# The head of a two-branch decoder layer: a first slice of one row tile, its modulation spread over column tiles, and bursts of four row tiles set among the transposes of x

## The chip, the cores and the metric

The kernel runs on one core of one Trainium2 chip. The metric is device time in microseconds of one execution. In the profile PE is TensorE (PEld its weight loads), DVE VectorE, ACT ScalarE, POOL GpSimd, and SP the queue from which nearly all weights are loaded.

## The reference

One layer is computed for 256 prompt tokens and 8 x 8 sample tokens that share all weights: T = 320 columns of tokens. What matters here is its beginning:

```
mod = jax.nn.silu(c) @ w_ada + b_ada
sh1, sc1, g1, sh2, sc2, g2 = [m[:, None, :] for m in jnp.split(mod, 6, axis=-1)]

h = _rmsnorm(x, norm1_g) * (1 + sc1) + sh1
p = h @ w_in
...
q, k, v, og, u, ga, gb, alr = jnp.split(p, idx, axis=-1)
```

c is one vector for the prompt and one for each of the 8 sample sequences, so 9 rows. D_MODEL is 2048: 16 row tiles of 128 channels. After p come gated linear attention in 4 heads, a pooling branch, a merge with w_o, and an FFN of inner width 5632. All in 32-bit floats.

## The kernel before

**Layout.** Activations lie transposed: channels on partitions, 320 tokens along the row. h has 16 row tiles, hh[k] (high part) and hl[k] (low part). A weight is split as well, into whi (a cast on ACT, L149) and wlo (a subtraction on DVE, L150), and each product is three matmuls of 320 columns (mm3, L163 to L165). A *unit* is 256 columns of w_in: two matmul groups, so 6 matmuls for each row tile of h. Its result lies in one of two PSUM tiles ("pm", two buffers) until `evac` copies it out.

**Slices.** h can't be formed at once, since each row tile needs its part of sh1 and sc1, and these need their columns of w_ada. So the first 15 units (all 11 of head 0, and 4 of gb for heads 1 and 3) are made slice by slice over row tiles: (0, 2), (2, 4), (4, 8), (8, 12), (12, 16). Each slice adds to what the ones before have left in SBUF. In slices of two row tiles, units with 512 neighbouring columns are made in pairs from one load (proj_pair). While a slice runs, the modulation and h of the next one are made in the background: a list `bg` of steps, of which `after_unit` runs as many as the count of units done so far asks for. The order of the steps is the order in which they are issued.

**Modulation.** HeadJob(b0, s) makes sh1 and sc1 of s row tiles. w_ada is the moving operand and silu(c) the weights (9 of 32 rows): 4 column tiles of PE work side by side, each on 64 s columns of w_ada. `load(k0)` issues two pieces of 512 KB (sections 0 and 1) for nk = 8 / s row tiles of w_ada; a *burst* (`burst(k0)`) first issues the loads of up to two bursts ahead and then runs its matmuls (ada_mm, L215). The pieces lie in eight buffers (tag "araw"). `finish` copies the sums to adasb, transposes them back and adds b_ada.

**Queues.** All loads of w_ada and w_in are issued on SP in program order (raw_chunk, L139; they are pinned with keep_in_program_order). A load waits there until its buffer is free, and those behind it wait too. w_in has three buffers (tag "raw"), the split parts five each. Other instructions are put in order by a scheduler unless they are pinned.

**The head.** c is transposed and turned into silu (scT); x (two tiles of the prompt, one of the samples) is loaded on SP, and its 16 row tiles are transposed on PE (L126) and copied out (L455); the sums of squares (ACT, L469) become rx, the inverse norm of each token on all partitions, by a matmul of a diagonal (dg, L477). Then comes HeadJob(0, 2), h of row tiles 0 and 1 (h_unit, L483 to L492), and the slices.

Of the kernel before, what the change touches and what calls it, by code (L numbers as in the profile page):

```python
# [11 lines left out]
F32 = mybir.dt.float32  # L12
# [8 lines left out]
P = 128  # L21
# [3 lines left out]
D = 2048  # L25
# [13 lines left out]
SLICES = ((0, 2), (2, 4), (4, 8), (8, 12), (12, 16))  # L39
# [41 lines left out]
def body(tc, A):  # L81
# [17 lines left out]
    def misc():  # L99
        return pmisc.tile([P, 512], F32, tag="m", name=nm("pm"))  # L100
# [23 lines left out]
    def tr(out, in_):  # L124
        k = in_.shape[0]
        PE.transpose(out, in_, ident[:k, :k])  # L126
# [26 lines left out]
    def split_chunk(src, nk, nn):  # L153
# [13 lines left out]
    def proj(w, col, k0, k1, xh, xl):  # L167

        ps = pmain.tile([P, 2, 512], F32, tag="pm", name=nm("ps"))
        for c0 in range(k0, k1, 4):  # L170
            nk = min(4, k1 - c0)
            for j, whi, wlo in split_chunk(w[:, c0:c0 + nk, col:col + 256], nk, 256):
# [21 lines left out]
    def proj_pair(w, col, k0, k1, xh, xl):  # L194

        parts = list(split_chunk(w[:, k0:k1, col:col + 512], k1 - k0, 512))
# [15 lines left out]
    def ada_mm(ps, k, raws, w):  # L212

        for j in range(4):
            ins = PE.matmul(ps[32 * j:32 * j + 32, 0:w], lhsT=scT[:, k, :], rhs=raws[j], start=k == 0,  # L215
                            stop=k == KT - 1, tile_position=(0, 32 * j))
            if j == 0:
                tc.keep_in_program_order(ins)
# [153 lines left out]
    with tc.tile_pool(name="head", bufs=1) as xp:  # L372
# [8 lines left out]
        nc.sync.dma_start(xn[2][0:TS], A["x_sample"].rearrange("b t d -> (b t) d"))  # L381
# [15 lines left out]
        V.tensor_tensor(scT[:, :, 0:9], crT, csig, op=ALU.mult)  # L397

# [3 lines left out]
        class HeadJob:  # L402
# [7 lines left out]
            def load(self, k0):  # L410
                if k0 >= KT or k0 in self.raws:
                    return
                c = self.b0 * P
                self.raws[k0] = [raw_chunk(wada[:, k0:k0 + self.nk, sec * D + c:sec * D + c + self.s * P], self.nk,
                                  self.s * P, xp, "araw", 8) for sec in range(2)]

            def burst(self, k0):
                for ahead in range(3):
                    self.load(k0 + ahead * self.nk)
                raws = self.raws[k0]  # L420
                self.raws[k0] = None
                if self.ps is None:
                    self.ps = misc()
                w = self.w
                for i in range(self.nk):
                    ada_mm(self.ps, k0 + i, [raws[j // 2][:, i, (j % 2) * w:(j % 2) * w + w] for j in range(4)], w)

            def finish(self):
                nb = self.s // 2
                sb = xp.tile([P, 2 * P], F32, tag="adasb", name=nm("adasb"))  # L430
                S.copy(sb[:, 0:self.w], self.ps[:, 0:self.w])
# [4 lines left out]
                for sec in range(2):  # L436
                    blk = sec * KT + self.b0
                    ada_out(mod[:, blk:blk + self.s, :], src[:, 2 * sec:2 * sec + 2, :, 0:9], blk, (2, nb))

            def steps(self):  # L440
                return ([lambda: self.load(0)] + [lambda k0=k0: self.burst(k0) for k0 in range(0, KT, self.nk)]
                        + [self.finish])


        xT = []
        for k in range(KT):
            pt = misc()
            for i in range(3):
                n = P if i < 2 else TS
                tr(pt[:, i * P:i * P + n], xn[i][:n, k * P:(k + 1) * P])  # L450
# [4 lines left out]
            (S.copy if k % 2 else V.tensor_copy)(xT[k], pt[:, 0:T])  # L455

        pt = misc()
# [7 lines left out]
        ssq = xp.tile([P, 3], F32, name="ssq")  # L465
        V.memset(ssq, 1.0)
        for i in range(3):
            n = P if i < 2 else TS
            S.activation(junk[:n], xn[i][:n], AF.Square, accum_out=ssq[:n, i:i + 1])  # L469
# [9 lines left out]
        V.tensor_copy(rx, prs[:, 0:T])  # L479

# [41 lines left out]
        for f in HeadJob(0, SLICES[0][1]).steps():  # L522
            f()
        for k in range(SLICES[0][1]):
            h_unit(k)
        for si, (k0, k1) in enumerate(SLICES):
            bg = []
            acc = 0 if si == 0 else 1
            if si + 1 < len(SLICES):
# [5 lines left out]
                bg += HeadJob(n0, n1 - n0).steps()  # L535
# [22 lines left out]
            while e < len(early):  # L558
                ge, kind, i, col = early[e]
                if k1 - k0 == 2 and kind not in "qku":  # L560
# [572 lines left out]
```

## Time and profile before

| what | us |
|---|---|
| median of 3 runs | 2017.34 |
| lowest and highest | 2016.09 to 2018.74 |
| the profiled execution | 2013.89 |
| its span, first to last instruction | 2012.1 |
| PE busy in it | 1958.5 |

The span is that of the profiled execution alone; the rest of its time lies around the span. In rows of a timeline the columns are start, duration, engine, line, operation, tiles and shape, and in brackets the idle time before and what ended it. In rows of windows they are the stretch, its length, busy time (and count) of PE, PEld, DVE, ACT and POOL, the granted clock of PE, the DMA share and GB/s. In rows of DMA issues they are the count, the size and the median time from issue to landing.

### The profile page before, as it was taken

To read this page: it belongs to the slowest core of one execution; us is meant where nothing else is said; L and a number is where in the kernel's file an instruction comes from. 1 tells how busy PE (TensorE), PEld (TensorE's weight loads), DVE (VectorE), ACT (ScalarE), POOL (GpSimd) and SP (SyncE) were. 2 spreads that over 40 slices of the span, in tenths; PEclk is the share of its full clock that TensorE was granted. 3 is DMA by queue.
4 is the path that set the end of the run, shared out by engine and by line. 5 is a ranking of instruction groups with operands and counts; after the bars stand their busy time and mean duration, and the time that the engine had idled before them with its cause. 6 is when DMAs were issued, how large, how long until landed. Compare 5 with 4: busy or idle time off the path is not lost.

```text
span 2012.1 us, 37187 instructions
## 1 busy us (share of the span) xinstructions
PE 1958.5 (97%) x15008; PEld 1851.2 (92%) x15008; DVE 1015.4 (50%) x1881; ACT 819.7 (41%) x1466; POOL 140.0 (7%) x261
## 2 busy tenths in 40 slices
PE   7999999999999999999989999999999999999997
PEld 5889998888898899888979999999999999999997
DVE  2556665465546433665574344444444444444554
ACT  4333374354335333643344333333333343444443
POOL 1112220111001100110020000000000000000000
PEclk9999999999999999999989999999999999999998
DMA  8888755776975887569736666544444554454442
GB/s 292 287 297 272 232 158 152 251 246 193 311 242 157 275 270 229 159 222 353 233 106 217 210 201 205 172 147 150 150 152 148 153 152 147 149 155 143 150 143 90
DMA packets 319598, 400.83 MB, mean 199 GB/s; under 512 B 13529, under 2 KB 259801, under 8 KB 319089
## 3 DMA queue, kind: packets, MB, share of 16 engines
q1 hardware_dynamic: 307154, 358.21, 56.1%
q0 software_dynamic: 12272, 40.25, 5.6%
q8 instruction: 117, 1.92, 0.4%
q14 instruction: 55, 0.45, 0.1%
HBM read 373.96 MB, written 24.67 MB: 198 GB/s over the span
## 4 chain that ended last, share of the span: by engine, by line
PE 92%; DMA 4%; DVE 1%; ACT 1%; issue 1%; SPq 0%; POOL 0%; ACTq 0%; POOLq 0%; DVEq 0%
PE ps L163 27%; PE ps L164 27%; PE ps L165 27%; PE pm L215 4%; DMA raw<-w_in 2%; PE pm L126 2%; DMA raw<-w_ada 2%; PE pm L797 1%; PE pm L766 1%; PE pm L818 1%; DVE wlo L150 1%; DMA xn<-x_sample 1%; PE pm L793 0%; PE pm L755 0%; PE pm L638 0%
## 5 line engine op out<-in xcount | busy, mean ns | idle before, releaser
L150 DVE TENSOR_TENSOR wlo<-raw,whi 128x512 fp32r<-128x512 f32 x952 | 659.4, 697 | 836.1 <-ACT whi L149 825.9
L149 ACT CAST whi<-raw 128x512 fp32r<-128x512 f32 x952 | 586.8, 621 | 1016.3 <-PE ps L164 868.6
L163 PE MATMUL ps<-hh,whi 128*128 128x320 f32 x1408 | 445.9, 317 | 6.9 <-ACT whi L149 2.8
L163 PE MATMUL ps<-h2h,whi 128*128 128x320 f32 x1408 | 437.6, 311 | 5.1 <-ACT h2h L1039 5.1
L165 PE MATMUL ps<-hh,wlo 128*128 128x320 f32 x1408 | 442.3, 314 | 0.3
L164 PE MATMUL ps<-hl,whi 128*128 128x320 f32 x1408 | 440.7, 313 | 0.4 <-DVE hl L492 0.4
L164 PE MATMUL ps<-h2l,whi 128*128 128x320 f32 x1408 | 435.2, 309 | 0.0
L165 PE MATMUL ps<-h2h,wlo 128*128 128x320 f32 x1408 | 435.2, 309 | 0.0
L163 PEld LDWEIGHTS ps<-hh,whi 128*128 128x128 f32 x1408 | 266.8, 190 | 30.2 <-issue 15.3
L165 PEld LDWEIGHTS ps<-hh,wlo 128*128 128x128 f32 x1408 | 266.9, 190 | 8.4 <-issue 5.7
L163 PEld LDWEIGHTS ps<-h2h,whi 128*128 128x128 f32 x1408 | 265.3, 189 | 9.3 <-ACT h2h L1039 6.1
L164 PEld LDWEIGHTS ps<-hl,whi 128*128 128x128 f32 x1408 | 266.9, 190 | 7.1 <-issue 5.4
L164 PEld LDWEIGHTS ps<-h2l,whi 128*128 128x128 f32 x1408 | 265.3, 188 | 0.0
L165 PEld LDWEIGHTS ps<-h2h,wlo 128*128 128x128 f32 x1408 | 265.2, 188 | 0.0
L163 PE MATMUL ps<-ah,whi 128*128 128x320 f32 x704 | 217.7, 309 | 0.0
L165 PE MATMUL ps<-ah,wlo 128*128 128x320 f32 x704 | 216.5, 308 | 0.0
L164 PE MATMUL ps<-al,whi 128*128 128x320 f32 x704 | 216.5, 308 | 0.0
L164 PEld LDWEIGHTS ps<-al,whi 128*128 128x128 f32 x704 | 132.0, 187 | 0.0
L163 PEld LDWEIGHTS ps<-ah,whi 128*128 128x128 f32 x704 | 132.0, 187 | 0.0
L165 PEld LDWEIGHTS ps<-ah,wlo 128*128 128x128 f32 x704 | 131.9, 187 | 0.0
L215 PE MATMUL pm<-raw,scT 128*32 128x128 f32 (+1 forms) x2688 | 110.6, 297 | 8.1 <-DMA raw<-w_ada 8.1
L215 PEld LDWEIGHTS pm<-raw,scT 128*32 128x32 f32 x2688 | 69.9, 111 | 35.9 <-issue 20.2
(279 smaller groups left out, 1539.6 us busy)
## 6 DMA issues: line engine op xcount, KB each, us to landing
raw<-w_ada SPq DMA_DIRECT2D x192, 512.0 KB, 6.0
raw<-w_gu SPq DMA_DIRECT2D x176, 512.0 KB, 3.6
raw<-w_in SPq DMA_DIRECT2D x173, 512.0 KB, 4.2
raw<-w_down SPq DMA_DIRECT2D x80, 512.0 KB, 3.4
S<-state_gla POOLq DMA_DIRECT2D x16, 1024.0 KB, 8.4
o_gs<-S POOLq DMA_DIRECT2D x16, 1024.0 KB, 5.7
raw<-w_o SPq DMA_DIRECT2D x32, 512.0 KB, 4.8
raw<-w_down SPq DMA_DIRECT2D x16, 256.0 KB, 2.6
```

The costliest lines, as they stand in the source:

```text
L126: PE.transpose(out, in_, ident[:k, :k])
L149: S.copy(hi, raw)
L150: V.tensor_sub(lo, raw, hi.bitcast(F32))
L163: PE.matmul(ps, lhsT=whi, rhs=xhi, start=start, stop=False)
L164: PE.matmul(ps, lhsT=whi, rhs=xlo, start=False, stop=False)
L165: PE.matmul(ps, lhsT=wlo, rhs=xhi, start=False, stop=stop)
L215: ins = PE.matmul(ps[32 * j:32 * j + 32, 0:w], lhsT=scT[:, k, :], rhs=raws[j], start=k == 0, stop=k == KT - 1, tile_position=(0, 32 * j))
L766: PE.matmul(pt, lhsT=E["kdn"][:, s, d * P:(d + 1) * P], rhs=E["vn"][:, s], start=s == 0, stop=s == 1)
L797: PE.matmul(pt[32 * j:32 * j + 32, :], lhsT=qeP[:, d, 4 * gg + j, :], rhs=E["S0", gg, d][:, j], start=False, stop=d == 1, tile_position=(0 ...
L818: PE.matmul(pt, lhsT=kpz[:, gg, j, d * P:(d + 1) * P], rhs=E["vp"][:, gg], start=True, stop=True)
```

## The change

The slices become (0, 1), (1, 3), (3, 7), (7, 11), (11, 16). The first has a job of its own kind, HeadJob1: one row tile, sections 0 and 1 and the two halves of the 16 row tiles of w_ada on the four column tiles, so that the halves are added afterwards; it is used for the last row tile too. A burst now always covers four row tiles. It issues the loads for itself and the next burst, runs its matmuls, and then issues the loads two bursts ahead. The first job's bursts are set among the transposes of x, which are pinned now with their copies; the last four row tiles are transposed in the first slice. The w_in pieces of the first five loads are split in program order around h of row tile 0. x_sample is loaded from POOL's queue, and Sqrt's table is loaded early by a dummy activation.

```diff
-SLICES = ((0, 2), (2, 4), (4, 8), (8, 12), (12, 16))
+SLICES = ((0, 1), (1, 3), (3, 7), (7, 11), (11, 16))
...
+        def hi(self):
+            tc.keep_in_program_order(S.copy(self.h, self.raw))
+
+        def lo(self):
+            tc.keep_in_program_order(V.tensor_sub(self.l, self.raw, self.h.bitcast(F32)))
...
-        nc.sync.dma_start(xn[2][0:TS], A["x_sample"].rearrange("b t d -> (b t) d"))
+        nc.gpsimd.dma_start(xn[2][0:TS], A["x_sample"].rearrange("b t d -> (b t) d"))
...
+        warm = xp.tile([P, 1], F32, name="warm")
+        S.activation(warm, csig[:, 0, 0:1], AF.Sqrt)
...
             def load(self, k0):
+
                 if k0 >= KT or k0 in self.raws:
                     return
                 c = self.b0 * P
-                self.raws[k0] = [raw_chunk(wada[:, k0:k0 + self.nk, sec * D + c:sec * D + c + self.s * P], self.nk,
-                                  self.s * P, xp, "araw", 8) for sec in range(2)]
+                self.raws[k0] = [[raw_chunk(wada[:, k:k + self.nk, sec * D + c:sec * D + c + self.s * P], self.nk,
+                                            self.s * P, xp, "araw", 8) for sec in range(2)]
+                                 for k in range(k0, k0 + 4, self.nk)]
 
             def burst(self, k0):
-                for ahead in range(3):
-                    self.load(k0 + ahead * self.nk)
-                raws = self.raws[k0]
+
+                self.load(k0)
+                self.load(k0 + 4)
+                pieces = self.raws[k0]
...
+                todo = [(p, i) for p in reversed(range(4 // self.nk)) for i in range(self.nk)]
+                for n, (p, i) in enumerate(todo):
+                    ada_mm(self.ps, k0 + p * self.nk + i,
+                           [pieces[p][j // 2][:, i, (j % 2) * w:(j % 2) * w + w] for j in range(4)], w,
+                           k0 == 0 and n == 0, k0 == KT - 4 and n == 3)
+                self.load(k0 + 8)
...
+        class HeadJob1:
...
+            def load(self, q):
+                if q in self.raws:
+                    return
+                c = self.b0 * P
+                self.raws[q] = [raw_chunk(wada[:, 8 * (j % 2) + 4 * q:8 * (j % 2) + 4 * q + 4,
+                                               (j // 2) * D + c:(j // 2) * D + c + P], 4, P, xp, "araw", 8)
+                                for j in range(4)]
...
+            def steps(self):
+                return [lambda: (self.load(0), self.load(1)), lambda: self.burst(0), lambda: self.burst(1), self.finish]
...
-        for f in HeadJob(0, SLICES[0][1]).steps():
-            f()
-        for k in range(SLICES[0][1]):
-            h_unit(k)
+        nx = SLICES[0][1]
+        for q, n in ((0, 8), (1, 10)):
+            job0.burst(q)
+            while len(xT) < n:
+                x_trans(len(xT), len(xT) % 2)
+        ew = []
+        for kind, i, col in units(0)[:6]:
+            if kind == "v" and i == 1:
+                continue
+            n = 512 if kind in ("v", "og") else 256
+            ready[col] = [EarlySplit(raw_chunk(win[:, 0:nx, col:col + n], nx, n))]
+            ew += ready[col]
+        ew[0].hi()
+        job0.finish()
+        h_first(0)
+        for k in (10, 11):
+            x_trans(k, 1)
+        ew[0].lo()
+        for e in ew[1:]:
+            e.hi()
+            e.lo()
...
-                bg += HeadJob(n0, n1 - n0).steps()
+                if si == 0:
+                    bg += [lambda k=k: x_trans(k, k % 2) for k in range(12, KT)]
+                b = n0
+                while b < n1:
+                    size = 4 if n1 - b >= 4 else 2 if n1 - b >= 2 else 1
+                    bg += (HeadJob(b, size) if size > 1 else HeadJob1(b)).steps()
+                    b += size
```

What this does to the order, at two places. The first is SP in the slice of four row tiles that comes third, (4, 8) before and (3, 7) now, from the first w_ada piece of its job on. The number behind raw tells the pieces apart; w_ada pieces are background, w_in pieces are units. Before:

```order
L139 DMA raw_1304<-w_ada 128x2x512
L139 DMA raw_1306<-w_ada 128x2x512
L139 DMA raw_1309<-w_in 128x4x256
L139 DMA raw_1344<-w_ada 128x2x512
L139 DMA raw_1346<-w_ada 128x2x512
L139 DMA raw_1348<-w_ada 128x2x512
L139 DMA raw_1350<-w_ada 128x2x512
L139 DMA raw_1362<-w_in 128x4x256
L139 DMA raw_1397<-w_ada 128x2x512
L139 DMA raw_1399<-w_ada 128x2x512
L139 DMA raw_1410<-w_in 128x4x256
L139 DMA raw_1447<-w_ada 128x2x512
```

The ninth piece of w_ada (raw_1447) takes over the buffer of the first (raw_1304). Now, from the fourth and last piece of the first load on:

```order
L139 DMA raw_1192<-w_ada 128x2x512
L139 DMA raw_1195<-w_in 128x4x256
L139 DMA raw_1231<-w_in 128x4x256
L139 DMA raw_1268<-w_ada 128x2x512
L139 DMA raw_1270<-w_ada 128x2x512
L139 DMA raw_1272<-w_ada 128x2x512
L139 DMA raw_1274<-w_ada 128x2x512
L139 DMA raw_1293<-w_ada 128x2x512
L139 DMA raw_1295<-w_ada 128x2x512
L139 DMA raw_1297<-w_ada 128x2x512
L139 DMA raw_1299<-w_ada 128x2x512
L139 DMA raw_1302<-w_in 128x4x256
```

raw_1293 to raw_1299 take over the buffers of the job's first four pieces, raw_1186 to raw_1192, and raw_1302 stands behind them. PE at the same place now, from the last rows of the burst that reads these four pieces to the first matmuls of the unit made of raw_1302 (whi_1304 and wlo_1305 are its first halves):

```order
L241 MATMUL pm_1276<-raw_1186,scT 32x256 x2
L241 MATMUL pm_1276<-raw_1188,scT 32x256 x2
L188 MATMUL ps_1301<-hh_88,whi_1304 128x320
L189 MATMUL ps_1301<-hl_965,whi_1304 128x320
L190 MATMUL ps_1301<-hh_88,wlo_1305 128x320
```

The burst stands directly ahead of that unit. Before, two units and two bursts stood between the burst that reads raw_1304 and the unit whose w_in piece comes behind raw_1447.

The second place is ACT at the start of the first slice. Before, the casts of the w_in pieces stood wherever the scheduler put them (raw_474 is the fourth piece, u's):

```order
L149 CAST whi_390<-raw_388 128x512
L149 CAST whi_410<-raw_408 128x512
L431 COPY adasb_360<-pm_291 128x128
L149 CAST whi_433<-raw_431 128x512
L149 CAST whi_437<-raw_431 128x512
L487 ACTIVATE hh_85<-xh_367,mod 128x256
L488 CAST hh_85<-xh_367 128x64
L487 ACTIVATE hh_86<-xh_377,mod 128x256
L488 CAST hh_86<-xh_377 128x64
L149 CAST whi_476<-raw_474 128x512
L346 ACTIVATE q_274<-ps_387 128x640
```

Now (raw_296 is q's piece, raw_300 k's, raw_304 v's, raw_308 u's):

```order
L166 CAST whi_298<-raw_296 128x256
L576 ACTIVATE hh_85<-xh_226,mod 128x256
L579 CAST hh_85<-xh_226 128x64
L534 COPY xT_337<-pm_333 128x320
L534 COPY xT_343<-pm_339 128x320
L166 CAST whi_302<-raw_300 128x256
L166 CAST whi_306<-raw_304 128x512
L166 CAST whi_310<-raw_308 128x256
L373 ACTIVATE q_228<-ps_354 128x640
```

The casts of k's and v's pieces now follow h of row tile 0 and two copies of transposes, and u's cast still stands ahead of q's copy. raw_308 takes over the buffer of raw_296, as there are three.

More of the change, by code (lines that the diff above doesn't have):

```diff
@@ L454, in body @@
                 xT.append(hp.tile([P, T], F32, tag="hl%d" % k, name="xT%d" % k))
-            (S.copy if k % 2 else V.tensor_copy)(xT[k], pt[:, 0:T])
+            pinned((S.copy if eng else V.tensor_copy)(xT[k], pt[:, 0:T]))
+        job0 = HeadJob1(0)
+        for q in range(2):
+            job0.load(q)
+        ssq = xp.tile([P, 3], F32, name="ssq")
+        V.memset(ssq, 1.0)
+        for i in range(3):
+            n = P if i < 2 else TS
+            S.activation(junk[:n], xn[i][:n], AF.Square, accum_out=ssq[:n, i:i + 1])
+        for k in range(SLICES[0][1]):
+            x_trans(k, 0)
         pt = misc()
```

90 lines of the change are left out of this document (70 added, 20 removed).

## The prediction

> **What bounds the kernel now.** I read the page first, then the timeline of the engines over the first 38 us, then the chain of waits, the clock by windows, and SP's own timeline where TensorE (PE) still waits later. The page:
>
> ```profile
> span 2012.1 us, 37187 instructions
> PE 1958.5 (97%) x15008; PEld 1851.2 (92%) x15008; DVE 1015.4 (50%) x1881; ACT 819.7 (41%) x1466; POOL 140.0 (7%) x261
> PE 92%; DMA 4%; DVE 1%; ACT 1%; issue 1%; SPq 0%; POOL 0%; ACTq 0%; POOLq 0%; DVEq 0%
> ```
>
> PE is the bound. The change takes no matmul away, so it can gain or lose only where PE waits, runs at a lower clock or switches between column tiles and full matmuls. The timeline of PE in the head:
>
> ```profile
> 10.45 1.12 PE L126 MATMUL pm<-cst,xn 128*128 128x128 f32 x4 [2.29 <-DMA xn<-x_prompt]
> 12.73 0.69 PE L126 MATMUL pm<-cst,xn 64*128 64x64 f32 x4 [1.16 <-DMA xn<-x_sample]
> 13.68 11.07 PE L126 MATMUL pm<-cst,xn 128*128 128x128 f32 x36 [0.26 <-DVE xT L455]
> 24.89 1.73 PE L477 MATMUL pm<-dg,cst 128*128 128x128 f32 x6
> 26.55 4.49 PE L215 MATMUL pm<-raw,scT 128*32 128x128 f32 x80
> 31.29 1.59 PE L215 MATMUL pm<-raw,scT 128*32 128x128 f32 x48
> 33.30 0.33 PE L126 MATMUL pm<-cst,adasb 128*128 128x128 f32 x1 [0.42 <-ACT adasb L431]
> 37.25 0.42 PE L164 MATMUL ps<-hl,whi 128*128 128x320 f32 x1 [0.39 <-DVE hl L492]
> ```
>
> Twelve row tiles of transposes take 11.07 us, 0.92 each. From 37.25 the main stream runs. Its matmuls start 0.15 us apart, but for a while 0.27 apart, as the chain and the windows show (the granted clock stands behind POOL, GB/s last):
>
> ```profile
> 40.49 0.27 PE ps L163
> 71.36 0.15 PE ps L164
> 34.90:38.30 3.40, 1.61 (x9) 1.35 (x10) 3.18 (x8) 1.72 (x5) 3.32 (x7) 1.00 0.99 304
> 38.30:41.70 3.40, 3.40 (x15) 3.40 (x14) 0.34 (x1) 0.37 (x1) 1.32 (x3) 0.50 1.01 309
> 41.70:45.10 3.40, 3.40 (x24) 3.33 (x23) 0.00 (x0) 1.74 (x3) 0.00 (x0) 0.99 1.04 399
> 1031.60:1045.20 13.60, 6.97 (x23) 6.07 (x24) 10.84 (x24) 6.17 (x19) 7.01 (x19) 0.50 0.03 8
> 14.40:17.80 3.40, 3.40 (x12) 1.78 (x12) 1.10 (x3) 3.15 (x8) 0.00 (x0) 1.00 1.09 386
> ```
>
> After a stretch of 3.4 us in which PE was half idle the granted clock is 0.50 for the next 3.4, and it comes back after a full one; behind the long idle time at 1031 it takes 13.6. At half clock 1 - 0.15/0.27 = 0.45 of the time is lost. The 1.00 at 14.4 is no record: the 80 column matmuls at 26.55 are 0.05 us apart and the 48 at 31.29 only 0.03, so PE ran at half speed until about 31.
>
> Last, how SP's queue couples to PE. A w_ada load waits on SP until the burst that reads its buffer is over, and everything behind it on SP waits too. PE and SP, then ACT and PE where that ended late, and SP and ACT once more:
>
> ```profile
> 75.62 1.00 PE pm L215 x16
> 76.62 0.35 PE ps L163
> 76.64 0.88 SPq L139 DMA_DIRECT2D raw<-w_ada  x2
> 77.62 0.42 SPq L139 DMA_DIRECT2D raw<-w_in  x1
> 83.16 1.14 ACT L149 CAST whi<-raw 128x512 fp32r<-128x512 f32 x2 [4.45 <-DMA raw<-w_in]
> 83.83 0.41 PE L163 MATMUL ps<-hh,whi 128*128 128x320 f32 x1 [1.25 <-ACT whi L149]
> 123.08 0.88 SPq L139 DMA_DIRECT2D raw<-w_ada  x2
> 124.05 0.42 SPq L139 DMA_DIRECT2D raw<-w_in  x1
> 129.87 1.14 ACT L149 CAST whi<-raw 128x512 fp32r<-128x512 f32 x2 [7.11 <-DMA raw<-w_in]
> PE ps L163 <- ACT whi L149: 2.8, 2, 1.6
> ```
>
> The burst ends at 76.62, SP issues two w_ada and one w_in at once, and the w_in is there at 83.16: 6.5 us for three pieces of 512 KB (6.8 from 123.08 to 129.87). PE had two units and two bursts to do meanwhile and waited 1.25; all such waits (last row) are 2.8.
>
> **The change, part by part.** *The blocked chunks.* Before, the load that waits for burst n stands two units and two bursts ahead of the unit whose w_in it delays. Now a burst of four row tiles reads four 512 KB pieces, and load(k0 + 8) stands right behind it in program order. Of eight buffers its four are those of that very burst, and the next unit's w_in stands behind the four on SP. PE has nothing between the burst and that unit. So each such load costs the whole way: 6.5 to 6.8 for three pieces, two more at 386 GB/s (2 x 0.524 MB / 0.386 = 2.7), then half of the 1.14 cast and the semaphores (83.83 - 83.16 = 0.67): 9.9 to 10.2, **10.0 us** of idle PE. Bounds: 9, if pieces follow closer, and 11.5, if spills share the engines. It happens for load(8) and load(12) of each four-tile job, that is in the slices over row tiles 1-2, 3-6 and 7-10: six times. Only behind the second one in slice 1-2 has PE something left, four matmuls (0.6) and a burst (2.0): minus 2.5. So 6 x 10.0 - 2.5 = **57.5**. The two-tile job fits its eight buffers and blocks nothing. The one-tile job in slice 7-10 lets its second four loads wait for the last burst of the job before, with a unit (24 x 0.15 = 3.6) and a transpose as cover: its first piece of 256 KB lands after 3.2 (a row below), three more at 0.7, the w_in 1.4, and 0.67 to PE: 7.3 less 3.8, **3.5**. Its rows are 512 bytes, a size that the trace of before does not show for w_ada; by bytes it is as said, by packets twice the time, 2.7 more. I take bytes.
>
> *The clock behind them.* After 10 us of idle time the clock is at 0.50 until a full 3.4 us stretch is busy: 1 to 2 stretches from PE's start, 5.1 us on average, of which 0.45 is lost: 2.3 (1.5 to 3.1). Six times: **13.8**.
>
> *The head.* Rows for it: POOL's first DMA issue and last of the early ones, a square, a table load and Sqrt on ACT, dg on DVE, the copy of q, 256 KB of w_in alone, four row tiles of transposes at full clock, a burst at full clock:
>
> ```profile
> 1.32 0.71 POOL L385 DMA_DIRECT2D vr<-b_ada  x1 [0.38 <-issue]
> 4.34 0.51 POOL L390 DMA_DIRECT2D vr<-gla_norm_g  x1
> 12.77 1.91 ACT L469 ACTIVATE junk<-xn 64x2048 f32<-64x2048 f32 x1 [0.28 <-DMA xn<-x_sample]
> 16.06 1.28 ACT L470 ACT_TABLE_LOAD   x1
> 17.36 0.30 ACT L470 ACTIVATE ssq<-ssq,epst 128x3 f32<-128x3 f32 x1
> 17.98 0.64 DVE L476 TENSOR_SCALAR dg<-cst,ssq 128x128 f32<-128x128 f32 x3
> 41.33 0.70 ACT L346 ACTIVATE q<-ps 128x640 f32<-128x640 f32 x1 [3.42 <-PE ps L165]
> raw<-w_in SPq DMA_DIRECT2D x6, 256.0 KB, 3.2
> 329.96 1.31 PE pm L126 x12
> 47.56 1.08 PE L215 MATMUL pm<-raw,scT 128*32 128x128 f32 x32
> ```
>
> x_sample moves from SP to POOL's queue, where it stands ahead of the others; the identity, which PE needs first, now comes behind all seven issues, at about 6. That is still ahead of x, so it costs nothing unless x lands before 8. The three x pieces share the engines; the last lands between 10.4 and 12.7, say 11.6, when ACT is just through with the first square and the table load moved up (8.4 + 2.0 + 1.3). Then ACT has two squares in a row, 4.0, to 15.6; Sqrt to dg is 0.6, the first dg 0.2: dg's matmuls, which PE has ahead of the second row tile, start at 16.5. Then 1.7 of them, nine row tiles at 0.92, 8.3, and two half-clock bursts of eight steps (80 records in 4.49 are 20 steps, 0.21 each without the last one's latency), 3.4: 29.9. The w_ada for them lands under the transposes, at half the rate too. From the adasb transpose to the stream it took 3.95 before; now, with h for one tile, 3.0 to 3.9, say 3.5: the stream starts at 33.4, 3.85 earlier. It then owes four row tiles' transposes (1.3 at full clock) and one block of w_ada (two bursts, 1.1 each): 3.5. So the early start is worth nothing by itself. New is that ACT's cast for u stands ahead of q's copy: u's w_in is issued only when the split of q's weights, now pinned behind h, frees a buffer, 33.8, and lands 3.2 later; cast 0.4, q's copy 0.7, and v, which needs q's PSUM tile, starts at 38.1, where PE was done with q and k at 36.2: plus 1.9. And the clock: transposes and lone bursts of 1.7 us did not raise it, so the stream starts at half clock, and then a unit of 1.6 us alternates with 0.92 of transposes. If transposes count as busy, full clock comes 1.5 stretches behind 38.1, at 43: 7.8 us of work x 0.45 = 3.5 lost. If not, 1.5 stretches behind the fourth, at 53: 8.0. The dip at 38.3 goes (3.4 x 0.45 = 1.5). So the head is 1.9 + 3.5 - 1.5 = +3.9 or 1.9 + 8.0 - 1.5 = +8.4; I take **+6**, since 11 us of nothing but transposes left PE at half clock in the row at 13.68, but no row has them mixed with units.
>
> The Trainium skill, "TensorE: Matmul & The Clock Gate", Part 4, states that transposes do not count as busy for the clock gate, which speaks against bursts set among transposes. By that the head would be +8.4 and the sum 2.4 higher; the row at 13.68 agrees.
>
> *Small terms.* 24 bursts of two row tiles become 12 of four; each switch saves about 0.2 (0.35 to the first matmul behind a burst, against 0.15): -2.4. The waits of before, 2.8, are replaced by the above: -2.8. The last slice has five tiles instead of four and no w_ada to load: 0. The splits and copies that change order on DVE (50% busy) and ACT (41%) lie beside PE; without that cover one copy, 0.7, would stand in a unit's way.
>
> **Sum.** 57.5 + 3.5 + 13.8 + 6 - 2.4 - 2.8 = +75.6. The profiled execution took 2013.89 (span 2012.1 and 1.8 around it): 2089.5. The median of the three runs is 2017.34, 3.45 above it: 2017.3 + 75.6 = **2093 us**.
>
> **Rivals.** (a) *The clock loses nothing behind the waits*: it drops and recovers while PE is idle, and transposes raise it in the head: 75.6 - 13.8 - 2.1 = +59.7, 2077. For it: the wait of 1.25 at 83.83 shows no drop. Against it: 13.6 us at 0.50 at 1031. (b) *The lookahead still suffices and the head holds its gain*, the faster side: SP issues the unit's w_in early enough. It decides at 10 us of PE work between the waiting load and the unit, some three units of 3.6; for it speaks that two units and two bursts left only 1.25 before, against it that the order has none now. Then no chunk is blocked, the stream warms in 1.5 stretches (2.3) and u is there in time: 2.3 - 1.5 - 5.2 = -4.4, 2013. (c) *The same, with the slow head*: +6 - 5.2, 2018.
>
> **Chances.** Forecast 0.83, (a) 0.08, (b) 0.05, (c) 0.04. Within the forecast: pieces 9 to 11.5 (-6, +9), clock (-5, +5), head (-2, +2), packets and a dip behind the last load (up to +5): taken together 2080 to 2114. With (a) and its own shorter pieces the range is 2065 to 2115. About 0.2% (4 us) is what a measurement of this kernel can tell from no change: faster by more is (b), within it (c).
>
> **What would show it.** Right: six idle times of PE of 9 to 11 us (one of 7 to 8) between 60 and 300 us, each just behind a burst and ended by ACT's cast of a w_in that SP issued behind four w_ada; clock 0.50 for 3.4 to 6.8 us behind each; the main stream from about 33, at half clock to 43 or 53. Wrong: the w_in behind a burst has landed when the burst ends. Then the stream's start and the clock of the first slice decide alone, and the time lies within 0.3% of before.

## The result, and the profile after

| kernel | median, us | runs | ratio to before, 95% interval |
|---|---|---|---|
| before | 2016.71 | 2014.64 to 2018.74 | |
| changed | 2088.36 | 2085.28 to 2093.15 | 1.0357 [1.0335, 1.0380] |

The change makes the kernel 3.6% slower: 71.6 us between the medians, 74.2 between the two profiled spans. (The median of the kernel before is now that of four runs.) The profiled execution of the changed kernel took 2088.07. Its page, the lines that answer to those shown of before, and one group row:

```profile
span 2086.3 us, 37281 instructions
PE 1970.1 (94%) x15009; PEld 1866.1 (89%) x15009; DVE 1018.9 (49%) x1899; ACT 816.3 (39%) x1472; POOL 140.4 (7%) x259
PE 90%; DMA 6%; ACT 1%; DVE 1%; issue 1%; SPq 0%; POOL 0%; ACTq 0%; POOLq 0%; DVEq 0%
L188 PE MATMUL ps<-hh,whi 128*128 128x320 f32 x1408 | 454.6, 323 | 63.9 <-ACT whi L149 56.2
```

PE is busy 11.6 us longer with one matmul more, so it ran slower somewhere, and it is idle for the rest. The last row says where: of 63.9 us idle in front of the first matmul of a triple, 56.2 were ended by ACT's cast of a weight. What PE waited for between 60 and 345 us (total, times, longest), the two longest rows:

```profile
PE ps L188 <- ACT whi L149: 56.2, 7, 9.5
PE ps L188 <- ACT hh L590: 2.5, 1, 2.5
```

Before, the first row was 2.8. One of the seven, from the timelines of PE, SP and ACT:

```profile
138.23 1.93 PE L241 MATMUL pm<-raw,scT 128*32 128x256 f32 x32
139.33 1.90 SPq L139 DMA_DIRECT2D raw<-w_ada  x4
141.33 0.57 SPq L139 DMA_DIRECT2D raw<-w_in  x1
148.61 1.14 ACT L149 CAST whi<-raw 128x512 fp32r<-128x512 f32 x2 [18.59 <-DMA raw<-w_in]
149.28 0.64 PE L188 MATMUL ps<-hh,whi 128*128 128x320 f32 x1 [9.11 <-ACT whi L149]
```

The whole coupling stands in these five rows. As the burst gives its buffers back, SP issues the four w_ada that waited for them (0.48 apiece) and only then the w_in; ACT can cast it at 148.61, 7.3 behind its own issue, and PE has stood for 9.11. From the first of the four issues to the unit it is 149.28 - 139.33 = 9.95; the issues begin 0.83 before the end of the burst (138.23 + 1.93 = 140.16), as its first buffer comes free. The windows around the same place (length, PE, PEld, DVE, ACT, POOL, clock, DMA share, GB/s), and the sum over the windows of half clock behind all seven waits:

```profile
129.40:139.70 10.30, 10.30 (x89) 9.58 (x91) 3.39 (x6) 0.61 (x1) 0.00 (x0) 1.00 0.17 65
139.70:142.30 2.60, 0.47 (x12) 0.00 (x0) 0.00 (x0) 0.00 (x0) 0.00 (x0) 1.00 0.69 180
142.30:152.50 10.20, 3.22 (x11) 3.00 (x12) 1.29 (x2) 1.14 (x2) 0.00 (x0) 0.50 0.56 211
sum 61.44, PE 27.97 PEld 27.07 DVE 17.80 ACT 16.55 POOL 2.08; mean PE 4.00 PEld 3.87 DVE 2.54 ACT 2.36 POOL 0.30
```

The DMA engines were 17% busy in the 10 us before the burst: there was room to load, and the loads stood waiting for their buffers. The clock stays at 0.50 for the first 3.2 us of PE's work. Over the seven places PE worked 27.97 us at half clock, of which 0.45 is lost: 12.6.

The head, PE's timeline (only the rows that matter) and the end of ACT's squares:

```profile
6.00 1.87 PE L126 MATMUL pm<-cst,junk 9*128 9x9 f32 x16 [6.00 <-POOL cst masks.py:199]
12.71 0.77 PE L126 MATMUL pm<-cst,xn 128*128 128x128 f32 x2 [2.64 <-DMA xn<-x_prompt]
15.10 1.91 ACT L543 ACTIVATE junk<-xn 64x2048 f32<-64x2048 f32 x1
18.17 1.84 PE L561 MATMUL pm<-dg,cst 128*128 128x128 f32 x6 [4.23 <-DVE dg L560]
19.94 3.73 PE L126 MATMUL pm<-cst,xn 128*128 128x128 f32 x12
23.60 1.94 PE L241 MATMUL pm<-raw,scT 128*32 128x128 f32 x32
25.47 2.10 PE L126 MATMUL pm<-cst,xn 128*128 128x128 f32 x9
27.49 1.08 PE L241 MATMUL pm<-raw,scT 128*32 128x128 f32 x32
32.46 0.41 PE L189 MATMUL ps<-hl,whi 128*128 128x320 f32 x1 [0.50 <-DVE hl L582]
35.98 0.63 PE L188 MATMUL ps<-hh,whi 128*128 128x320 f32 x1 [0.71 <-ACT q L373]
57.84 0.41 PE L188 MATMUL ps<-hh,whi 128*128 128x320 f32 x1 [0.97 <-DVE mg L375]
61.52 0.90 PE L188 MATMUL ps<-hh,whi 128*128 128x320 f32 x2 [2.53 <-ACT hh L590]
```

```profile
33.07:36.48 3.41, 2.70 (x11) 2.30 (x10) 1.05 (x3) 1.36 (x3) 0.00 (x0) 0.50 0.76 219
36.48:39.90 3.42, 3.42 (x14) 2.93 (x14) 1.19 (x2) 1.57 (x3) 0.00 (x0) 0.50 1.01 318
39.90:43.31 3.41, 3.41 (x23) 2.91 (x21) 2.27 (x5) 1.53 (x3) 0.00 (x0) 1.00 1.06 367
60.38:67.20 6.82, 5.68 (x21) 5.66 (x22) 2.34 (x7) 1.81 (x5) 3.41 (x8) 0.50 1.05 394
```

No clock record lies before 26.24, where the first one reads 1.0; before it the bursts tell, since one of 32 column matmuls takes 1.94 at 23.60 and 1.08 at 27.49. So the clock came up between bursts and transposes, fell again at the stream's start (33.07) and was back at 39.90. At 61.52 PE waits for h of row tiles 1 and 2, and another stretch of half clock lies around it.

### The profile page after: what moved, and what is told of

The parts are those of the page before. It is cut to its first block, busy times and chain, and to the rows that moved or that the text cites. A ratio compares the mean times of both kernels' runs of the same rounds, so it can differ in the third digit from the quotient of the medians.

```text
span 2086.3 us, 37281 instructions
## 1 busy us (share of the span) xinstructions
PE 1970.1 (94%) x15009; PEld 1866.1 (89%) x15009; DVE 1018.9 (49%) x1899; ACT 816.3 (39%) x1472; POOL 140.4 (7%) x259
## 4 chain that ended last, share of the span: by engine, by line
PE 90%; DMA 6%; ACT 1%; DVE 1%; issue 1%; SPq 0%; POOL 0%; ACTq 0%; POOLq 0%; DVEq 0%
PE ps L188 27%; PE ps L189 26%; PE ps L190 26%; PE pm L241 4%; DMA raw<-w_in 3%; DMA raw<-w_ada 2%; PE pm L126 2%; PE pm L923 1%; PE pm L892 1%; PE pm L944 1%; DVE wlo L150 0%; ACT whi L149 0%; DMA xn<-x_prompt 0%; PE pm L919 0%; SPq L139 0%
## 5 line engine op out<-in xcount | busy, mean ns | idle before, releaser
L150 DVE TENSOR_TENSOR wlo<-raw,whi 128x512 fp32r<-128x512 f32 (+1 forms) x956 | 659.1, 693 | 869.0 <-ACT whi L149 861.7
L149 ACT CAST whi<-raw 128x512 fp32r<-128x512 f32 (+1 forms) x956 | 587.0, 618 | 1082.5 <-PE ps L189 891.5
L188 PE MATMUL ps<-hh,whi 128*128 128x320 f32 x1408 | 454.6, 323 | 63.9 <-ACT whi L149 56.2
L190 PE MATMUL ps<-hh,wlo 128*128 128x320 f32 x1408 | 448.8, 319 | 0.2 <-DVE wlo L150 0.2
L189 PE MATMUL ps<-hl,whi 128*128 128x320 f32 x1408 | 448.2, 318 | 0.5 <-DVE hl L582 0.5
L188 PEld LDWEIGHTS ps<-hh,whi 128*128 128x128 f32 x1408 | 273.9, 195 | 85.9 <-ACT whi L149 60.6
L189 PEld LDWEIGHTS ps<-hl,whi 128*128 128x128 f32 x1408 | 274.2, 195 | 7.2 <-issue 5.4
L190 PEld LDWEIGHTS ps<-hh,wlo 128*128 128x128 f32 x1408 | 273.1, 194 | 7.3 <-issue 5.3
```

Of the source, the lines that this page charges most:

```text
L149: S.copy(hi, raw)
L150: V.tensor_sub(lo, raw, hi.bitcast(F32))
L188: PE.matmul(ps, lhsT=whi, rhs=xhi, start=start, stop=False)
L189: PE.matmul(ps, lhsT=whi, rhs=xlo, start=False, stop=False)
L190: PE.matmul(ps, lhsT=wlo, rhs=xhi, start=False, stop=stop)
```

## The experiments

Theory T: a w_in that stands behind waiting w_ada loads on SP's queue is late by the way of four pieces and one w_in, less the work that PE has in between. Against it stand: the DMA engines are full whatever the queue; the bursts of four, the slices or the clock cost the time by themselves. Twelve kernels were run, each timed beside the kernel before.

| run | median, us | ratio to before, 95% interval |
|---|---|---|
| e1_pool_queue | 2026.42 | 1.0056 [1.0041, 1.0071] |
| e2_load_late | 2045.16 | 1.0152 [1.0133, 1.0171] |
| e3_oldburst | 2030.35 | 1.0075 [1.0057, 1.0092] |
| e4_burst4 | 2074.08 | 1.0293 [1.0270, 1.0316] |
| e5_dg_late | 2026.15 | 1.0058 [1.0043, 1.0073] |
| e6_bg_early | 2027.22 | 1.0068 [1.0050, 1.0087] |
| e7_all | 2032.45 | 1.0089 [1.0074, 1.0104] |
| e8_before_mm | 2027.66 | 1.0072 [1.0056, 1.0089] |
| e9_before_pool4 | 2022.14 | 1.0046 [1.0030, 1.0062] |
| e10_before_pool | 2023.32 | 1.0054 [1.0040, 1.0068] |
| e11_xs_sp | 2024.51 | 1.0059 [1.0041, 1.0077] |
| e12_spaced | 2020.44 | 1.0024 [1.0016, 1.0033] |

**e1_pool_queue: take w_in out from behind the loads.**

```diff
-                                            self.s * P, xp, "araw", 8) for sec in range(2)]
+                                            self.s * P, xp, "araw", 8, nc.gpsimd) for sec in range(2)]
```

(raw_chunk issues on the queue given; HeadJob1 likewise where it is not the first job.)

> The changed kernel with one edit: all w_ada loads of the head but those of the first slice are issued on GpSimd's queue instead of SP's, into the same eight buffers, so they still wait for the same bursts, but no w_in stands behind them. Theory (the w_in is late because it stands behind waiting loads in SP's queue): the six idle times of PE behind bursts (52.8 in all, and 3.65 in front of the one-tile job) go, and so does the half clock behind them (about 11 + 1.5): 2088 - 69 = 2019, 2015 to 2030 since w_in and w_ada now share the DMA engines. Rival A (the four pieces fill the DMA engines, whatever queue they come from): a w_in in flight beside four pieces lands about as late, half of the waits or more stay: 2050 or above. Rival B (the bursts of four themselves, or the clock, cost the time, not the wait): 2075 or above.

PE's longest waits between 60 and 345 us:

```profile
PE ps L188 <- ACT hh L592: 3.5, 2, 2.2
PE pm L241 <- DMA raw<-w_ada: 1.3, 1, 1.3
```

No wait for a weight's cast is left in that stretch, and none of the half-clock windows behind them. The loads still wait for the same bursts, in the same eight buffers, and the bursts of four and the new slices are all there: some 61 us (3.57% over before against 0.56%) went by changing who stands behind whom. Rivals A and B fall. The 0.56% that is left may in part be the price of the other queue; e10_before_pool measures that.

**e2_load_late: a dose of cover.**

```diff
-                self.load(k0 + 8)
```

> The changed kernel without the load behind each burst of four: each load of four pieces now stands in front of the next burst, one step later in program order, still on SP. Theory: the wait is the way of four pieces and one w_in (9.5) less the work that PE has between the burst that frees the buffers and the unit behind the load. That work was nothing and is now a unit of 3.6 and a burst of 2.1: 9.5 - 5.7 = 3.8 each, so six waits of about 4 in place of 9.5, and somewhat less half clock: 2088 - 34 - 3 = 2051, 2040 to 2060. Rival A (DMA engines full): no change by the order, 2080 or above. Rival C (any lookahead at all suffices): the waits go, 2025 or below.

One of the places, and the sum of such waits:

```profile
130.91 1.93 PE L241 MATMUL pm<-raw,scT 128*32 128x256 f32 x32
132.01 1.90 SPq L139 DMA_DIRECT2D raw<-w_ada  x4
136.49 1.93 PE L241 MATMUL pm<-raw,scT 128*32 128x256 f32 x32
143.18 0.63 PE L188 MATMUL ps<-hh,whi 128*128 128x320 f32 x1 [4.75 <-ACT whi L149]
PE ps L188 <- ACT whi L149: 17.7, 5, 4.9
```

SP issues the four loads 1.1 us after the start of the first burst, as in the changed kernel (139.33 after 138.23). But the w_in behind them now belongs to the unit after next, and PE has a unit and a burst to do meanwhile. The wait is 4.75 in place of 9.1; 3.8 was expected. The whole way is somewhat longer here, 143.18 - 132.01 = 11.2 instead of 9.95. So the wait is the way less the cover, and the cover can be dosed. Six waits of about 4 were expected, 24 in all; five came, 17.7.

**e4_burst4: the one part alone, in the kernel before.** The edit is the diff's `load`, `burst` and `steps` in the old kernel, with the old slices and the old head:

```diff
-                for ahead in range(3):
-                    self.load(k0 + ahead * self.nk)
-                raws = self.raws[k0]
+                self.load(k0)
+                self.load(k0 + 4)
+                pieces = self.raws[k0]
...
+                self.load(k0 + 8)
```

> The kernel before with the new job for w_ada alone: bursts of four row tiles and the load behind the burst; slices, first slice and the order of the head stay old. Theory: the three four-tile jobs (row tiles 4-7, 8-11, 12-15) block two loads each: six waits of about 9.5, about 11 lost at half clock behind them, 2.7 less for switches, 2.8 of old waits gone: 2017 + 57 + 11 - 5.5 = 2079, 2068 to 2090. Rival (the waits come only with the new head or slices): 2040 or below.

```profile
PE ps L163 <- ACT whi L149: 52.2, 6, 9.5
```

Six waits of up to 9.5, with nothing of the new head or slices: the load behind the burst of four is enough by itself.

**e3_oldburst: the reverse**, the changed kernel with the old job:

```diff
-                self.load(k0)
-                self.load(k0 + 4)
-                pieces = self.raws[k0]
+                for ahead in range(3):
+                    self.load(k0 + ahead * self.nk)
+                raws = self.raws[k0]
...
-                self.load(k0 + 8)
```

> The changed kernel with the old job for w_ada: bursts of two row tiles, loads three bursts ahead; slices, first slice and early splits stay new. Theory: what is left is the head. Against the kernel before: the first slice ends about 6.8 later by the traces, and the one-tile job's block may stay (3.65 + 1.5); bursts and waits are as before: 2017 + 6.8 + 5 = 2029, 2020 to 2035. Rival (the new slices cost the time, by themselves): above 2060. Rival (the head's loss is made good later): 2017 or below.

```profile
PE ps L188 <- ACT whi L149: 8.0, 5, 3.6
```

It is 0.75% over before, as expected. The old lookahead doesn't fit the new slices quite as well (8.0 of these waits, 2.8 in the kernel before). The rest of the 15.6 us, in the head and the new slices, was not taken apart.

**e5_dg_late, e11_xs_sp, e6_bg_early: what the head's parts are worth**, each an edit of e1_pool_queue: four row tiles' transposes ahead of the dg matmuls; x_sample back on SP; background work two units earlier in the first two slices.

```diff
         prs = misc()
+        while len(xT) < 5:
+            x_trans(len(xT), len(xT) % 2)
```

```diff
-        nc.gpsimd.dma_start(xn[2][0:TS], A["x_sample"].rearrange("b t d -> (b t) d"))
+        nc.sync.dma_start(xn[2][0:TS], A["x_sample"].rearrange("b t d -> (b t) d"))
```

```diff
-                want = len(bg) * count[1] // len(early)
+                want = min(len(bg), len(bg) * (count[1] + (2 if si < 2 else 0)) // len(early))
```

(The first diff leaves the loop out at its old place; in e6 each job also loads its first eight pieces at its start, and in each slice this load stands first among the steps.)

> The kernel of e1_pool_queue (w_ada of the head on GpSimd's queue) with one edit more: the transposes of row tiles 1 to 4 stand ahead of the three dg matmuls in program order. There PE waited 4.4 for dg while these four tiles, 3.74 at half clock, had been ready. Theory (the head loses through PE's program order): dg's matmuls start at 18.4 as before with the four tiles behind PE, the stream starts 3.7 earlier, at about 29.6, and the time falls by 3 to 4 against e1, to about 2023. Rival (the first slice is bound by the landing of w_ada or of u's w_in): bursts or u then wait, and the time stays at 2026.

> The kernel of e1_pool_queue with x_sample back on SP's queue, behind the two pieces of x_prompt, and so the identity back at the front of GpSimd's. Theory on the head (x_sample beside x_prompt makes x_prompt land at 9.6 and 12.7 instead of 7.0 and 10.5, so that ACT has two squares in a row behind 12.7): dg's matmuls start at about 16 instead of 18.4 and the stream 2.4 earlier. In time, either 2024 (the head's gain holds) or, as in the run with the dg matmuls moved, 2026 (a stream that starts 2.5 earlier gives it back at small waits behind 100 us).

> The kernel of e1_pool_queue with the work beside the first two slices two units earlier, and each job's first eight loads at its start. Theory: the waits for h at the ends of the first two slices (1.6, 0.9, 2.5), for adasb (0.9) and for w_ada at the first burst of row tiles 3 to 6 (1.6) go, 7.5 in all: 2019, 2017 to 2023. Rival (what is late there is bandwidth, so that another wait takes their place): 2024 or above.

In e5 and e11 the stream starts earlier, at 30.81 and 31.24 instead of 33.30 (in e11 dg's matmuls start at 15.81, as expected), and the time doesn't follow: the three ratios lie within 0.03% of each other. In e5 the profile shows the lead of 2.4 at 60 us used up at three short waits, at 108 (0.49), 126 (0.99, of which each time 0.15 is normal spacing) and 191 (1.05). What paces PE there, so that a lead of 2 us doesn't last, was not found. In e6 some of the waits for h went, and others came, above all these two (the third row is ACT's timeline ahead of the first):

```profile
PE ps L188 <- DVE k L371: 3.3, 1, 3.3
PE ps L188 <- ACT k L373: 2.1, 1, 2.1
177.12 1.14 ACT L149 CAST whi<-raw 128x512 fp32r<-128x512 f32 x2 [5.88 <-DMA raw<-w_in]
```

The first stands at 180. Eight w_ada, four other loads and the spills had been issued one behind the other on GpSimd's queue from 156.5 on. A w_in that SP issued among them, at 158.5, took 11.5 to land; those that it issued from 141 to 156 took 3.7. ACT had waited 5.88 for one more w_in, to 177.1, and k's copy stands on DVE behind the split of that weight. What I expected of e5 and e6 failed. In e6 these rows fit the rival that was named: loads that are issued earlier share the DMA engines with another transfer and make it late. For e5 no reason is shown.

**e8_before_mm and e7_all: does the kind of matmul set the clock?** In e8 the kernel before transposes x by ordinary matmuls; e7 is e1 with this and the edits of e5 and e6.

```diff
-                tr(pt[:, i * P:i * P + n], xn[i][:n, k * P:(k + 1) * P])
+                PE.matmul(pt[:, i * P:i * P + n], lhsT=xn[i][:n, k * P:(k + 1) * P], rhs=ident[:n, :n], start=True, stop=True)
```

> The kernel before with one edit: the 48 transposes of x are issued as ordinary matmuls with the identity, of the same size. Theory (transposes do not raise the clock, matmuls do): it is at full at 17 to 21 instead of 31.3, 10 to 14 us at half clock are saved, times 0.45: 5 to 6 less, 2009, unless w_ada's landing then bounds the head. Rival (transposes count like matmuls, and the clock was late for another reason): the timeline of the head is the same and so is the time, 2015.

> The kernel of e1_pool_queue with the edits of e5 and e6 and one more: the transposes of x are issued as ordinary matmuls with the identity as the moving operand, of the same size. Theory: 3.7 and 7.5 from the two edits, and some 3 to 5 because ordinary matmuls raise the clock at about 18 to 21 where it was half until 30: 2026 - 11 - 4 = 2011, 2005 to 2018, so it is no slower than the kernel before. Rival (the clock rises no earlier): 2015.

PE's timeline in the head of e8:

```profile
10.81 25.17 PE L450 MATMUL pm<-cst,xn 128*128 128x128 f32 x88 [1.68 <-DMA xn<-x_prompt]
36.24 1.77 PE L477 MATMUL pm<-dg,cst 128*128 128x128 f32 x6
37.94 5.58 PE L215 MATMUL pm<-raw,scT 128*32 128x128 f32 x128
```

Theory and rival of e8 both fall. Each ordinary 32-bit matmul is recorded as two passes, so 44 of them take 25.17, 0.57 each, where a transpose took 0.31: that costs the 11 us by which the stream is late. And 25 us of them back to back didn't raise the clock either: its first record is at 41.85, during the bursts, and the first bursts behind them (89 records in the 4.26 us from 37.94) are still 0.05 apart, as at half clock before. e7 is slower than e1, 2032 us where 2011 was expected and 2015 by the rival; there 12 such matmuls take 7.07 at 15.36.

**e10_before_pool and e9_before_pool4: what GpSimd's queue costs, and what bursts of four are worth.** The edit of e1 in the kernel before, and in e4:

```diff
-                                  self.s * P, xp, "araw", 8) for sec in range(2)]
+                                  self.s * P, xp, "araw", 8, nc.gpsimd if self.b0 else None) for sec in range(2)]
```

> The kernel before with the w_ada loads of all jobs but the first on GpSimd's queue, and bursts of two as they were. Theory: only the old waits for w_in go: 2014.5 - 2.8 = 2012, 2009 to 2014. If e9 is 2 to 4 below this one, the bursts of four are worth what their switches save. Rival (shared engines): 2014 or above.

> The kernel before with the bursts of four (as in e4_burst4) and the w_ada loads of all jobs but the first on GpSimd's queue (as in e1_pool_queue). Theory: no w_in stands behind a waiting load, so nothing of e4's loss is left, and what the bursts of four are worth shows alone: 12 switches of 0.23 saved, 2.7, and the old waits for w_in, 2.8, gone: 2014.5 - 5.5 = 2009, 2006 to 2013, faster than the kernel before. Rival (with w_ada on another queue its pieces and the w_in share the DMA engines, and other waits take the place): 2014 or above.

Both forecasts fail, and both rivals (2014 or above) hold. e10 is slower than before though its waits for a weight's cast (2.8) are gone. The DMA issues of w_ada between 60 and 310 us, before and in e10; the two waits of PE between 60 and 345 that are new in e10; and ACT ahead of the first of them, which stands at 82.08:

```profile
raw<-w_ada SPq DMA_DIRECT2D x49, 512.0 KB, 5.8
raw<-w_ada POOLq DMA_DIRECT2D x48, 512.0 KB, 7.4
PE ps L163 <- DVE v L344: 2.6, 2, 2.3
PE ps L163 <- ACT hh L488: 2.3, 1, 2.3
79.86 1.14 ACT L149 CAST whi<-raw 128x512 fp32r<-128x512 f32 x2 [5.43 <-DMA raw<-w_in]
```

A piece takes 1.6 longer to land from GpSimd's queue, and each issue holds GpSimd for 0.71 (eight of them from 70.26: 5.69), where it took 0.48 on SP in the changed kernel. The Trainium skill, "DMA: Bandwidth & Descriptors", section "SWDGE vs HWDGE vs iDMA", calls the path from SP and ACT faster to set up than GpSimd's; the 0.71 against 0.48 agrees. But the wait at 82.08 comes from sharing: the w_in that SP issued at 70.84, beside those eight w_ada, took 8.9 to land (the median of w_in in that stretch is 5.0), ACT cast it at 79.86, and v's copy on DVE stands behind its split. For the wait for h, at 116.01, no reason is shown. So the other queue has a price of its own, 0.54%. How much of e1's 0.56% is that price stays open: e3, with all loads on SP, loses 0.75%, so the new slices cost something too. Whether bursts of four save their switches isn't settled: e9 is 1.2 us below e10, with overlapping intervals, where 2 to 4 were expected.

**e12_spaced: the cure on SP itself**, e4 with each waiting load about three units behind its burst.

```diff
-                bg += HeadJob(n0, n1 - n0).steps()
-                bg += [lambda k=k: h_unit(k) for k in range(n0, n1)]
...
+                    bg += [lambda j=j, f=first: (f(), j.load(0)), lambda j=j: j.load(4), lambda j=j: j.burst(0), lambda j=j: j.burst(4),
+                           none, lambda j=j: j.load(8), lambda j=j: j.load(12), none,
+                           lambda j=j: j.burst(8), lambda j=j: j.burst(12), j.finish]
```

> The kernel of e4_burst4 (before with bursts of four), all on SP's queue, with the steps of each four-tile job put at fixed units: load 0, load 4, burst 0, burst 4, a unit without a step, load 8, load 12, another, burst 8, burst 12, finish, then h. Each load that waits for a burst now stands three units behind it in program order instead of right behind it. Theory (the wait is 9.5 less the work that PE has between the freeing burst and the unit behind the load): three units of 3.6 cover it in the slices of four row tiles; in the slice of two, where a unit is half as long, one or two waits of 1 to 4 stay. Of e4's 60 over before some 55 to 65 go: 2074 - 60 = 2014, 2008 to 2020. Rival (spacing alone does not do, the pieces fill the DMA engines at any place): 2035 or above.

The waits between 20 and 345 us, and the place of the one long wait:

```profile
PE ps L163 <- ACT whi L149: 8.6, 5, 6.0
79.83 1.93 PE L216 MATMUL pm<-raw,scT 128*32 128x256 f32 x32
77.10 6.46 SPq L139 DMA_DIRECT2D raw<-w_ada  x8
93.25 0.64 PE L163 MATMUL ps<-hh,whi 128*128 128x320 f32 x1 [6.01 <-ACT whi L149]
```

Of e4's 52.2 there are 8.6 left, and 6.0 of them is one wait, in the slice of two row tiles: a unit is half as long there, and both loads, eight pieces, go in front of the same w_in. In the slices of four row tiles no wait is over 0.9. The ratio falls from 1.0293 to 1.0024, and the time to 2020.44, just beyond what was expected (2014, 2008 to 2020); no kernel here beats the one before.

## Why the prediction was right, point by point

When three of the matmuls of 320 columns start in the profiled executions, in us for before and as the difference to it for the others (counted from 0): 1200, in the last slice, behind all bursts of the slices; 1600, behind all slices; and the last of its kind:

```
matmul    before    changed   e1        e3        e4        e12
1200      260.45    +73.66    +12.70    +18.58    +55.93    +4.23
1600      336.56    +68.81    +7.85     +12.21    +57.18    +5.44
11433     1995.87   +74.28    +9.97     +16.06    +58.65    +7.37
```

**The blocked chunks** (57.5 + 3.5 = 61.0): measured 56.2 in seven waits, as many as forecast and at the places forecast. The five full ones are 9.2 on average instead of 10.0 (8.9 to 9.5), the shorter one 6.6 instead of 7.5. The way itself was right: from the first of the four issues to the unit it is 10.0 on average. What the forecast left out is that the issues begin 0.84 before the end of the burst. Shown by e1 (gone without the queue), e2 (17.7 left under a unit and a burst of cover) and e4 (there without anything else). For the one-tile job 3.73 was measured at 267.79 against 3.5, but the two parts were both longer than forecast: the way 8.5 (from SP's issue at 259.26) and the cover 4.8 (from there to the end of PE's work at 264.05). The forecast way was 7.3 by bytes and 10.0 by packets, so the choice between them isn't settled, and the nearness of the term is luck. Its row:

```profile
267.79 0.42 PE L188 MATMUL ps<-hh,whi 128*128 128x320 f32 x1 [3.73 <-ACT whi L149]
```

**The clock behind them** (13.8): 27.97 x 0.45 = 12.6, of which 11.1 behind the six (4.1 us of work each at half clock, where 5.1 was taken) and 1.5 behind the one-tile job's, a dip that stood only in my range. Rival (a), that nothing is lost, is wrong: 9 us of idle time is enough for the drop, and so is the 3.73 of the one-tile job, behind which the clock was 0.50 from 268.59 to 272.00.

**The waits of before and the switches** (-2.8 and -2.4): the first is replaced, as forecast: before, PE waited for a weight's cast only twice between 60 and 345. For a burst of four the rows give 2.10 from the matmul before to the matmul behind it, against 1.24 for one of two: 2 x (1.24 - 0.15) - (2.10 - 0.15) = 0.23 saved, 12 times, 2.7. In total times it isn't shown (e9 against e10).

**The head** (+6): what is left of the 68.81 is 68.8 - (56.2 - 2.8) - 12.6 + 2.7 = 5.5. That the size came out right is luck. By matmul 1200 the same sum leaves 73.7 - 53.4 - 12.6 + 2.7 = 10.4 for the head and the early slices, and the 4.8 between 1200 and 1600 were given back at the end of the last slice and just behind it, which the prediction put at 0. The waits of PE there, two rows of before and one of the changed kernel, and a window of before that has no counterpart:

```profile
PE psy L163 <- ACT q L346: 3.4, 1, 3.4
PE pm L638 <- DVE w L625: 1.4, 1, 1.4
PE psy L188 <- ACT q L373: 2.2, 1, 2.2
284.08:287.50 3.42, 3.42 (x15) 3.42 (x14) 1.70 (x3) 3.39 (x5) 0.42 (x1) 0.50 0.67 206
```

That is 2.6 of waits and 3.42 x 0.45 = 1.5 of half clock; why they are shorter wasn't found. e1 and e3, which have the new slices, get 4.9 and 6.4 back there; e4 and e12, which have the old ones, lose 1.2. In the head itself:
- dg's matmuls started at 18.17, not 16.5. The first square started at 9.65 instead of 8.4, so ACT was through with it and the table load only at 13.08, when the last piece of x_prompt (12.71) was there too, and two squares follow (the second is the row at 15.10, 1.91).
- The stream started at 32.46, not 33.4, in spite of that. The step "transposes and lone bursts of 1.7 us did not raise it" was wrong; no row of before has bursts among transposes. Here they raised the clock at 26.24, and between 26.4 and 31.9 in the runs of e1, e2, e3, e5, e6 and e11. So the transpose of adasb stood at 29.65 and not, with dg late, at 31.6; from there to the stream it was 2.8 instead of 3.5.
- v waited 0.71 for q's copy, not 1.9.
- The half clock at the stream ended at 39.90, not at 43 or 53: (2.70 + 3.42) x 0.45 = 2.8 lost, not 3.5 or 8.0. A stretch in which units and transposes alternate was enough. The Trainium skill, "TensorE: Matmul & The Clock Gate", Part 4, says that full clock doesn't engage for transposes, which don't count as PE-busy in the same way. As the prediction read it, no stretch with transposes in it counts, and the stream would have stayed at half to 53; the row at 39.90 disagrees with that reading. It doesn't show that transposes count, since three quarters of the stretch from 36.48 were units. For transposes alone before's 11 us agree with the page, but in e8 ordinary matmuls of the same tiles did no better, so the kind of instruction is not what told there.
- Not foreseen at all: h of row tiles 1 and 2 is late at 61.52 (2.53, and 0.97 for mg at 57.84), with 5.68 x 0.45 = 2.6 of half clock behind it. The first slice has half the work of the old one, and thirteen background steps stand in it; that this makes h late is an argument, no run shows it. These 6.1 are more than the lines above saved: 0.9 at the stream's start, 1.2 at v and 2.8 of the half clock that was taken (6 - 1.9 + 1.5 = 5.6). 6 - 4.9 + 6.1 = 7.2 of the 10.4; the other 3.2 were not traced.

**The rest.** The last 5.5 of the 74.3 come behind 400 us, where both kernels run the same code; the other kernels lose 1 to 4 there too against this execution of before. The medians are 71.6 apart, so some 2.6 of it belong to the two single executions; what the rest is stays open. **Rivals (b) and (c)**, that the lookahead suffices: it needed some 10 us of PE's work between the waiting load and the unit. e2 with 5.7 waits 4.75 and e12 with about 10.7 waits at most 0.9, so the point from which it decides was set about right; the changed kernel has 0 there. **What would show it:** the signs came, a little short: one of the five full waits is 8.9 (9 to 11 was named) and the shorter one 6.6 (7 to 8).

## What to carry to other kernels

On a queue that issues in order, a load that waits for a buffer is as much a barrier for what stands behind it as for itself: cost each such load as the way of everything up to the next urgent piece, less the work between the instruction that frees the buffer and the one that needs that piece. Making the batch larger with the same number of buffers takes the lookahead away, and what cured it best here is to put the load a full way's worth of work behind the burst (e12, 0.24% over before); another queue takes the wait away too, but e10 pays 0.54% for that queue alone. A lead at the start of a kernel is worth only what no later wait takes back: look for that wait before counting on it.

## What the runs showed of the hardware that was not expected

- Transposing by an ordinary 32-bit matmul with the identity took 0.57 us a tile (25.17 for 44), a transpose 0.31 (11.07 for 36), both at half clock by the spacing of the bursts behind them.
- Neither 11 us of transposes nor 25 us of such matmuls, back to back, raised the granted clock. In the changed kernel a burst of 1.94 among transposes was followed by full clock at 26.24. In e1 the stretch from 23.34 to 26.75, with a burst of 1.93 among transposes, was not, and full clock came at 30.16, during the second burst. What the clock counts was not found.
- Between 60 and 310 us, 512 KB of w_ada from GpSimd's queue landed in 7.4 us (median, e10) and held POOL for 0.71 each, against 5.8 (before) and 0.48 (changed kernel) on SP.
- A wait of 3.73 us was enough for a stretch of half clock behind it, as much as waits of 9; a wait of 1.25, at 83.83 in the kernel before, was not.
